# Moving weight accumulations, token sums, splits and additions in a one-core hybrid transformer layer, and tying two transposes to later product steps

## The chip, the cores and the metric

The kernel runs on one core of one Trainium2 chip. The metric is the device time of one execution in microseconds (us). The core has TensorE (PE, matrix products), VectorE (DVE), ScalarE (ACT), GpSimd (POOL) and SyncE (SP, which here only issues DMAs). PE writes into PSUM banks; everything else works in SBUF. A DMA that adds to its destination (`accum_op`) is issued by POOL, plain ones mostly by SP.

## The reference, cut to what matters

All arrays are float32; L = 1024 tokens, D = 1024, 256 context tokens, one layer.

```
h      = rms_norm(x) * (1 + sc1) + sh1          # modulated by c
r, d   = split_heads(h @ w_in)                  # 4 retention heads, 4 differential heads
y_ret  = silu(g) * (both directions of chunkwise retention, group-normed)
y_diff = subln(softmax(q1 k1) v - lam * softmax(q2 k2) v)
x      = x + g1 * (concat(y_ret, y_diff) @ w_out)
h2     = rms_norm(x) * (1 + sc2) + sh2
a, b   = split(conv3(h2 @ w_up))
x      = x + g2 * ((silu(a) * b) @ w_down)
return rms_norm(x)
```

## The kernel before, in words

**Precision.** Every large product is made from three TensorE passes (`passes`, lines 130 to 135): high by high, high by low, low by high. So each operand is split: ACT casts the high part, and DVE (or POOL) subtracts it from the raw values to give the low part. One call of `passes` is three matmuls and is called a step here; a `product` is four steps.

**Strassen forms.** The out projection (tokens times `w_out`) and the up and down projections use seven half-size products in place of eight. Their operands are sums of blocks. `A11, A12, A21, A22` are the four blocks of `w_out`; the sums of them live in DRAM: `ws_d[0] = A21 + A22`, `ws_d[1] = A11 + ws_d[0]`, `ws_d[2] = A11 + A21`, `ws_d[3] = A12 + ws_d[1]`. First SP copies one block into each (lines 808 and 810), then POOL adds the other with accumulating DMAs in two halves of 512 KB each (`weight_sum`, line 366). The sums of token blocks live in `t1_d` to `t4_d` (in the profile `sgd`), the second half of the retention rows in `yr_d` (`yrd`).

**Stages around the change.**

1. Query projection (up to about 445 us). PE makes `pl` products; beside it the generator `outputs()` runs the 16 head pairs of retention. A `Pair` loads its keys `rk` (line 257) and values `kvo` on SP, `score` makes `pc` (line 269), POOL forms `qq`, DVE `sc`, PE `po`, ACT squares, POOL takes a power (line 288), DVE normalizes (293), POOL adds and gates (295, 296), PE transposes (301), ACT copies to `yr`, and SP writes it out (309). For the second half of the tokens POOL also accumulates `yr` into `t1_d` (line 311). After some pairs `weight_sum` issues its DMAs.
2. Attention (about 445 to 650 us). 32 units (4 heads of 8 query tiles) run as a software pipeline written out by hand; in step n unit n begins its scores. Its order on PE, DVE, ACT and SP is fixed (`in_order`). POOL makes each unit's power (line 987, `pool_ins`), and issues loads and sums "after" the `pool_ins` of the unit five steps back: query and key loads for unit n + 3 (lines 1018, 1021), `joined_tokens` (an addition and one or two accumulating DMAs, lines 1130 and 1132), the copy `t2_d <- t1_d` (1150), and one slice of the out weights (`wo_gen`, line 1100). SP copies `t2_d` to `t4_d` per head at steps 14, 21 and 29 (1152).
3. Out projection (about 640 to 728 us). `out_step` makes the products; `weights` loads, casts and subtracts a block of weights (1106 and 1107), `sum_operand` does so for token sums (1336 and 1337; for `t4_d`, the last head is added up from two parts at line 1333), and `gate` multiplies a result by `g1` (1345) and adds it to `x1` (1346). Rows 0 to 3 are `rows0`, rows 4 to 7 `rows1`; `left` and `right` are column halves. `freed` is the last of the four gates of `rows0`, `left`.
4. `norm2` normalizes a finished row tile (ACT squares at 1226, DVE 115, POOL power 116, DVE scaling 1231). `turned` transposes a column of row tiles on PE (1238) into one PSUM bank, once for the first four tiles (`turned0`) and once for the last four (`turned1`); the copies out of it (1240, 1242) are split (1245 and 1246) and combined (1423, 1426) into the operands B11 to B22 and T1 to T4.
5. Up projection. The first three blocks' `chain` and `second` products stand ahead of the loop, with `turned1` beside them, one of its pieces after every few steps; then `fifth` (reads T1) and `third` (reads B22), then the `chain` products that read T2, T3, T4.

**What sets the order.** Within `in_order` sections it is the order of the program. Elsewhere a planner orders each engine's instructions when the kernel is built, from the dependencies, the order of the program and its own costs. `order_only(a, b)` tells it to put a behind b on their common engine; it makes no wait on the chip. `issue_after` does so for DMA issues. `last_turn[1, d]` is the last row tile's transpose for column d.

Of the kernel before, what the change touches and what calls it, by code (L numbers as in the profile page):

```python
# [12 lines left out]
ALU = mybir.AluOpType  # L13
# [4 lines left out]
P = 128  # L18
# [56 lines left out]
def kernel(  # L75
# [85 lines left out]
    with ExitStack() as p1:  # L161
# [89 lines left out]
        class Pair:  # L251
# [46 lines left out]
            def turn(self, behind=None):  # L298
                pt = tr_tile([P, 2, P], "pyt")
                for s in range(2):  # L300
                    ins = nc.tensor.transpose(pt[:, s, :], self.y[:, s, :], ident)
                    if behind is not None:
                        order_only(ins.ins, behind.ins)
                left = H * NT // 2 - 1 - (self.h * NT // 2 + self.g)
                yr = rt.tile([P, 2, P], F32, name="yr") if left > 1 else rt.tile([P, 2, 2, P], F32, name="yr", tag=("qq", "sc")[left])[:, 0]
                second, o = self.g // 2, self.g % 2 * 2 * P
                nc.scalar.mul(yr, pt, 1.0 if second else -1.0)
                for to in (yr_d,) if second else (t3_d, t1_d):
                    nc.sync.dma_start(out=to[:, self.h, o : o + 2 * P].rearrange("p (s l) -> p s l", s=2), in_=yr)
                if second:  # L310
                    nc.gpsimd.dma_start(out=t1_d[:, self.h, o : o + 2 * P].rearrange("p (s l) -> p s l", s=2), in_=yr, accum_op=ALU.add)

        keyed, key_copies = [], []
# [44 lines left out]
                    last[d] = dst  # L358
                yield

        w_terms = [(i, a, k) for i, a in ((0, A22), (2, A21), (1, ws_d[0]), (3, ws_d[1])) for k in (0, 2)]

        def weight_sum(after):
            if w_terms:
# [4 lines left out]
        def outputs():  # L369
            n_pairs, per_head = H * NT // 2, NT // 2  # L370
            pairs, more = {}, states((2, 3))
            for n in range(-2, n_pairs + 3):
                if n + 2 < n_pairs:
                    pairs[n + 2] = Pair(n + 2)
                if n == -2:
                    continue
                if n + 1 < n_pairs:
                    pairs[n + 1].score()
                forming = per_head <= n < 3 * per_head
                if n == per_head - 1 or forming and n % 2 == 0:  # L380
                    next(more)
                yield
                if 0 <= n < n_pairs:
                    pairs[n].output(0)
                yield
                if forming:
                    next(more)
                yield
                if n == n_pairs + 2:
                    for _ in range(4):  # L390
                        yield
                    pairs[n - 3].turn(newest[0])
                elif n >= 3:
                    pairs[n - 3].turn()
                if 0 <= n < n_pairs:
                    pairs[n].output(1)
                    pairs[n].squares()
                yield
                if 0 <= n - 1 < n_pairs:
                    pairs[n - 1].gate()  # L400
                    for _ in range({1: 2, 2: 2, 10: 1, 11: 1, 12: 1, 13: 1}.get(n, 0)):
                        weight_sum(last_y[0])
                if forming:
                    next(more)
                yield
                yield
# [684 lines left out]

    g1 = wo.tile([P, D], F32, name="g1")

    def out_weights(srcs, sl, eng=nc.sync, low=nc.vector, lag=0, after=()):
        raws = []
        srcs = [src[:, k, :] for src in srcs for k in range(4)]
        for k in range(len(srcs) + lag):
            if k < len(srcs):
                raw = wo.tile([P, 512], F32, name="woraw", bufs=5)
                wo_loads.append(eng.dma_start(out=raw, in_=srcs[k]))  # L1100
                raws.append(raw)
            yield
            if k >= lag:
                whi = wo.tile([P, 512], F32R, name="wohi", bufs=8)
                wlo = wo.tile([P, 512], F32R, name="wolo", bufs=8)
                wo_casts.append(nc.scalar.copy(whi, raws[k - lag]))
                part = low.tensor_tensor(out=wlo, in0=raws[k - lag], in1=r32(whi), op=ALU.subtract)
                for ins in after:
                    order_only(part.ins, ins.ins)
                sl.append((whi, wlo))  # L1110

# [22 lines left out]
    with ExitStack() as p2:  # L1134
        at = p2.enter_context(tc.tile_pool(name="at", bufs=2, reuse_waits="tile"))
        psa = p2.enter_context(tc.tile_pool(name="psa", bufs=1, space=PSUM, reuse_waits="tile"))

        turns = {}
        start = len(nc.cur_bb.bb.instructions)
        order = sorted(TAU.items(), key=lambda it: it[1] % 1.0)  # L1140
        for n in range(n_units + 8):
            if 2 < n < n_units:
                units[n] = Unit(n)
                vars(units[n]).update(fore[n])
            if n == 9:
                with tc.issue_after(units[n - 5].pool_ins.ins):
                    nc.gpsimd.dma_start(out=g1, in_=row_d[0].rearrange("p c -> (p c)").partition_broadcast(P))
            if n == 8:
                with tc.issue_after(units[n - 5].pool_ins.ins):
                    nc.gpsimd.dma_start(out=t2_d[:, :, :], in_=t1_d[:, :, :])  # L1150
            if n in (14, 21, 29):
                nc.sync.dma_start(out=t4_d[:, (14, 21, 29).index(n), :], in_=t2_d[:, (14, 21, 29).index(n), :])
            for half, when in ((0, (11, 18, 26, 33)), (1, (16, 24, 31))):
                if n in when:
                    with tc.issue_after(units[min(n - 5, n_units - 1)].pool_ins.ins):
                        joined_tokens(when.index(n), half)
            for op, t in order:
                u = n - int(t)
                if 0 <= u < n_units and (u > 1 or op not in EARLY) and (op, u) not in MOVED:
                    turns[op, u] = len(nc.cur_bb.bb.instructions)  # L1160
                    units[u].run(op)
                    turns[op, u] = nc.cur_bb.bb.instructions[turns[op, u]]
                for o, v in MOVED.get((op, u), ()):
                    units[v].run(o)
                if op == "f" and n >= 9 and n not in (11, 16, 18, 24, 26, 31, 33):
                    with tc.issue_after(units[min(n - 6, n_units - 1)].pool_ins.ins):
                        next(wo_gen, None)
            if n + 3 < n_units:
                after = units[n - 5].pool_ins if n >= 5 else last_va[0]
# [148 lines left out]
        for _ in g:  # L1318
            pass

    def weights(src, *after):
        sl = []
        run(out_weights((src,), sl, after=after))
        return sl

    def sum_operand(src, tt, half, turn=False, after=()):
        raw = raw0[:, 4 * half : 4 * half + 4, :]
        n = H if src is not t4_d else H - 1
        nc.sync.dma_start(out=raw[:, :n, :], in_=src[:, :n, :])
        if n < H:  # L1330
            nc.sync.dma_start(out=raw[:, 3, :], in_=t2_d[:, 3, :])
            for a in range(2):
                nc.gpsimd.tensor_tensor(out=raw[:, 3, :], in0=raw[:, 3, :], in1=r32(yT[a][1][:, D // P - 1, :]), op=ALU.add)
        sign, parts = -1.0 if turn else 1.0, []
        for k in range(H):
            cast = nc.scalar.mul(tt[0][:, k, :], raw[:, k, :], sign)
            part = nc.vector.scalar_tensor_tensor(out=tt[1][:, k, :], in0=raw[:, k, :], scalar=sign, in1=r32(tt[0][:, k, :]), op0=ALU.mult, op1=ALU.subtract)
            for ins in after:
                order_only(part.ins, ins.ins)
            parts.append(part)  # L1340
        return parts
# [37 lines left out]
    for t in range(4):  # L1379
        freed = gate(rows0[t], c1[t], left, ALU.add)  # L1380
        done(t, left)
    w4 = weights(A22, freed)
    sum_operand(t4_d, Y12, 1, after=(freed,))
    raws = [up_load(j) for j in range(NSUM)]
    halves = [(a[:, 0:4, :], a[:, 4:8, :], b[:, 0:4, :], b[:, 4:8, :]) for a, b in raws]
    for a1, a2, b1, b2 in halves:
# [12 lines left out]
    w2 = weights(A12)  # L1399
    beside(turned0(), 0.36, -3.0)  # L1400
    for t in out_step(c1, Y12, w4, False, True, True):
        gate(rows1[t], c1[t], right, ALU.subtract, nc.gpsimd)
        done(4 + t, right)
    c1 = [(psB if t < 2 else psC).tile([P, 512], F32, name=f"o3_{t}", tag="bank") for t in range(4)]
    for t in out_step(c1, Y22, w2, True, True, True):
# [62 lines left out]
    for j in range(NPRE):  # L1468
# [460 lines left out]
```

## Time and profile before

| | us |
|---|---|
| runs | 1374.64, 1375.2, 1376.37 (median 1375.2) |
| profiled execution | 1374.97 |
| its span, first to last instruction | 1373.2 |
| PE busy | 1350.2 |
| DVE busy | 1001.5 |
| ACT busy | 749.1 |
| POOL busy | 351.8 |
| mean granted TensorE clock | 0.998 of full |

In a timeline row stand the start and the length in us, the engine, the line of the kernel, the operation, what is written from what, shapes and a count; in brackets, how long the engine sat idle before it and whose end released it. Rows that merge several instructions give the time from the first start to the last end. Consecutive PE and DVE operations overlap a little, so the distance from one start to the next is shorter than an operation's length. SPq and POOLq rows are DMA issues. A row of a stretch gives for each engine its busy time and its count of instructions, then the granted clock, the mean share in which the 16 DMA engines were busy, and GB/s. A row of a wait gives the total, the number of times and the longest.

### The profile page before, as it was taken

The numbers are of one execution on the slowest core, as the hardware profiler recorded it, in microseconds if no ns is written. First come the engines' busy times: TensorE is split into PE (matmuls) and PEld (weight loads), VectorE is DVE, ScalarE is ACT, GpSimd is POOL, SyncE is SP. The second block draws the span as 40 slices with busy tenths as digits, with TensorE's granted clock in tenths as the row PEclk, the third lists the DMA queues.
The fourth block names the chain that finished last, engine by engine and source line by source line (L and its number), as shares of the span: only waits on it lengthen the run. The fifth ranks groups of instructions, "written<-read, shape, count | busy, mean of one in ns | idle before, by whom it ended". The sixth has DMA issues, their size and how long they took to land.

```text
span 1373.2 us, 19870 instructions
## 1 busy us (share of the span) xinstructions
PE 1350.2 (98%) x6978; PEld 1134.5 (83%) x6978; DVE 1001.5 (73%) x1508; ACT 749.1 (55%) x1429; POOL 351.8 (26%) x440
## 2 busy tenths in 40 slices
PE   9999999999999999999999999999999999999997
PEld 6788888888888799988877888888888888888886
DVE  4746874425775898997889986777766777798857
ACT  4643312434665789987437654455554555455543
POOL 1210005403777435543131222212222210000001
PEclk9999999999999999999999999999999999999999
DMA  9567897655877877745853898988888875963523
GB/s 362 218 252 245 288 325 232 202 171 157 212 199 189 186 168 141 145 93 154 333 165 92 200 224 218 232 223 214 208 221 215 208 193 171 375 217 110 176 92 123
DMA packets 130636, 279.71 MB, mean 204 GB/s; under 512 B 13716, under 2 KB 35220, under 8 KB 129624
## 3 DMA queue, kind: packets, MB, share of 16 engines
q1 hardware_dynamic: 100440, 212.99, 45.6%
q0 software_dynamic: 29520, 64.00, 25.4%
q10 hardware_dynamic: 576, 1.44, 0.3%
q8 instruction: 55, 0.90, 0.3%
q14 instruction: 45, 0.37, 0.1%
HBM read 212.04 MB, written 69.75 MB: 205 GB/s over the span
## 4 chain that ended last, share of the span: by engine, by line
PE 81%; DVE 7%; ACT 4%; POOL 3%; issue 3%; DMA 2%; SPq 0%; POOLq 0%; DVEq 0%; ACTq 0%
PE chain L133 6%; PE chain L134 6%; PE chain L135 6%; PE c L134 5%; PE c L133 5%; PE c L135 5%; PE pv L972 4%; PE pA L940 4%; PE pn L135 3%; PE pn L134 3%; PE pn L133 3%; PE pl L133 3%; PE pl L135 3%; PE pl L134 3%; PE third L133 3%; PE third L135 3%
## 5 line engine op out<-in xcount | busy, mean ns | idle before, releaser
L1263 POOL DMA_DIRECT2D cmb<-w_up x80 | 73.6, 1142 | 175.1 <-DMA cmb<-w_up 141.7
L133 PE MATMUL pl<-hT,whi 128*128 128x512 f32 x256 | 105.4, 412 | 0.0
L133 PE MATMUL chain<-T,whi 128*128 128x512 f32 x264 | 103.1, 391 | 0.0
L134 PE MATMUL chain<-T,whi 128*128 128x512 f32 x264 | 102.8, 389 | 0.0
L135 PE MATMUL chain<-T,wlo 128*128 128x512 f32 x264 | 102.2, 389 | 0.0
L943 DVE TENSOR_REDUCE mt<-pA 128x1 f32<-128x1280 f32 x64 | 95.2, 1488 | 7.5 <-PE pA L940 6.3
L135 PE MATMUL pl<-hT,wlo 128*128 128x512 f32 x256 | 100.1, 391 | 0.0
L134 PE MATMUL pl<-hT,whi 128*128 128x512 f32 x256 | 99.9, 390 | 0.0
L947 ACT ACTIVATE p<-pA,mt 128x1280 f32<-128x1280 f32 x64 | 85.5, 1336 | 11.2 <-DVE mt L943 9.1
L940 PE MATMUL pA<-ks,qhl 128*128 128x512 f32 (+1 forms) x384 | 89.6, 368 | 1.3 <-DMA ks<-dk 0.8
L133 PE MATMUL c<-whi,ghl 128*128 128x512 f32 x232 | 90.2, 389 | 0.0
L134 PE MATMUL c<-wlo,ghl 128*128 128x512 f32 x232 | 90.2, 389 | 0.0
L135 PE MATMUL c<-whi,ghl 128*128 128x512 f32 x232 | 90.2, 389 | 0.0
L1187 ACT CAST whi<-cmb 128x512 fp32r<-128x512 f32 x60 | 37.4, 625 | 83.0 <-PE chain L134 65.1
L940 PEld LDWEIGHTS pA<-ks,qhl 128*128 128x128 f32 x384 | 67.9, 189 | 13.7 <-DVE mt L943 1.2
L972 PE MATMUL pv<-va,aT 128*128 128x128 f32 x640 | 77.4, 276 | 1.3 <-DVE yT L1001 1.0
L972 PEld LDWEIGHTS pv<-va,aT 128*128 128x128 f32 x640 | 74.0, 192 | 3.0 <-DVE yT L1001 2.1
L1187 ACT CAST whi<-wra 128x512 fp32r<-128x512 f32 x54 | 33.0, 622 | 71.7 <-PE third L134 42.3
L134 PE MATMUL third<-yT,whi 128*128 128x512 f32 x168 | 65.4, 389 | 0.0
L133 PE MATMUL third<-yT,whi 128*128 128x512 f32 x168 | 65.4, 389 | 0.0
L135 PE MATMUL third<-yT,wlo 128*128 128x512 f32 x168 | 65.4, 389 | 0.0
L133 PE MATMUL pn<-whi,hT 128*128 128x512 f32 x160 | 64.8, 405 | 0.0
(342 smaller groups left out, 3854.6 us busy)
## 6 DMA issues: line engine op xcount, KB each, us to landing
cmb<-w_up POOLq DMA_DIRECT2D x80, 256.0 KB, 6.5
wm<-w_mod SPq DMA_DIRECT2D x32, 512.0 KB, 5.7
cmb<-w_up SPq DMA_DIRECT2D x60, 256.0 KB, 5.4
raw<-w_in SPq DMA_DIRECT2D x27, 512.0 KB, 5.4
wra<-w_up SPq DMA_DIRECT2D x23, 512.0 KB, 6.2
W<-w_down SPq DMA_DIRECT2D x44, 256.0 KB, 5.5
wrb<-w_up SPq DMA_DIRECT2D x40, 256.0 KB, 3.8
ad<-s SPq DMA_DIRECT2D x20, 512.0 KB, 5.8
```

The source lines that it names most:

```text
L133: mm(ps, lh, rh, start=first, stop=False, skip_group_check=more)
L134: mm(ps, lh, rl, start=False, stop=False, skip_group_check=more)
L135: return mm(ps, ll, rh, start=False, stop=last, skip_group_check=more)
L940: mm(self.pa[m][:, c0:c1], self.q[:, m, i, qs], self.k[:, m, c0:c1], start=(i == 0), stop=(i == 1))
L943: nc.vector.tensor_reduce(out=self.mt[:, m : m + 1], in_=self.pa[m][:, :LK], axis=AX.X, op=ALU.min)
L947: nc.scalar.activation(self.p[m], self.pa[m][:, :LK], AF.Exp, scale=-1.0, bias=self.mt[:, m : m + 1], accum_out=self.s[:, m : m + 1])
L972: mm(self.pv, self.aT[:, c, :], self.v[:, c, :], start=(c == 0), stop=(c == NKT - 1))
L1187: cast = nc.scalar.copy(hi, src)
L1263: nc.gpsimd.dma_start(out=o, in_=src, accum_op=ALU.add)
```

## The change

- The four accumulations `ws_d[1] += ws_d[0]` and `ws_d[3] += ws_d[1]` are issued no longer after pairs 9 to 12 but in steps 15, 17, 21 and 28 of attention.
- The last head's two accumulations of `yr` into `t1_d` are left out; step 6 of attention does both at once, from `yr_d`, in DRAM. The copy `t2_d <- t1_d` goes from step 8 to 9, the first join from 11 to 12; a weight slice is taken at 11 and not at 12.
- For the fourth block of out weights (`w4`) and for `t4_d`, the first two of four subtractions need not follow `freed`.
- Six additions go from POOL to DVE: two in `sum_operand`, four in the gates of `rows1`, `right`.
- The transposes `last_turn[1, 0]` and `last_turn[1, 4]` were put behind the third and fourth step of block 0's `second`; they are put behind the second and third step of block 1's `chain`.

```diff
-                if second:
+                if second and self.h < H - 1:
                     nc.gpsimd.dma_start(out=t1_d[...], in_=yr, accum_op=ALU.add)
...
-        w_terms = [(i, a, k) for i, a in ((0, A22), (2, A21), (1, ws_d[0]), (3, ws_d[1])) for k in (0, 2)]
+        w_terms = [(i, a, k) for i, a in ((0, A22), (2, A21)) for k in (0, 2)]
...
-                    for _ in range({1: 2, 2: 2, 10: 1, 11: 1, 12: 1, 13: 1}.get(n, 0)):
+                    for _ in range({1: 2, 2: 2}.get(n, 0)):
...
-    def out_weights(srcs, sl, eng=nc.sync, low=nc.vector, lag=0, after=()):
+    def out_weights(srcs, sl, eng=nc.sync, low=nc.vector, lag=0, after=(), free=0):
...
-                for ins in after:
+                for ins in after if k - lag >= free else ():
                     order_only(part.ins, ins.ins)
...
-            if n == 8:
+            if n in (6, 9, 15, 17, 21, 28):
                 with tc.issue_after(units[n - 5].pool_ins.ins):
-                    nc.gpsimd.dma_start(out=t2_d[:, :, :], in_=t1_d[:, :, :])
+                    if n == 6:
+                        nc.gpsimd.dma_start(out=t1_d[:, H - 1, :], in_=yr_d[:, H - 1, :], accum_op=ALU.add)
+                    elif n == 9:
+                        nc.gpsimd.dma_start(out=t2_d[:, :, :], in_=t1_d[:, :, :])
+                    else:
+                        i, j, k = {15: (1, 0, 0), 17: (1, 0, 2), 21: (3, 1, 0), 28: (3, 1, 2)}[n]
+                        nc.gpsimd.dma_start(out=ws_d[i][:, k : k + 2, :], in_=ws_d[j][:, k : k + 2, :], accum_op=ALU.add)
...
-            for half, when in ((0, (11, 18, 26, 33)), (1, (16, 24, 31))):
+            for half, when in ((0, (12, 18, 26, 33)), (1, (16, 24, 31))):
...
-                if op == "f" and n >= 9 and n not in (11, 16, 18, 24, 26, 31, 33):
+                if op == "f" and n >= 9 and n not in (12, 16, 18, 24, 26, 31, 33):
...
-    def sum_operand(src, tt, half, turn=False, after=()):
+    def sum_operand(src, tt, half, turn=False, after=(), free=0):
...
-                nc.gpsimd.tensor_tensor(out=raw[:, 3, :], in0=raw[:, 3, :], in1=..., op=ALU.add)
+                nc.vector.tensor_tensor(out=raw[:, 3, :], in0=raw[:, 3, :], in1=..., op=ALU.add)
...
-            for ins in after:
+            for ins in after if k >= free else ():
                 order_only(part.ins, ins.ins)
...
-    w4 = weights(A22, freed)
-    sum_operand(t4_d, Y12, 1, after=(freed,))
+    w4 = weights(A22, freed, free=2)
+    sum_operand(t4_d, Y12, 1, after=(freed,), free=2)
...
-        gate(rows1[t], c1[t], right, ALU.subtract, nc.gpsimd)
+        gate(rows1[t], c1[t], right, ALU.subtract)
...
-        if j == 0:
-            order_only(last_turn[1, 0].ins, steps[-2].ins)
-            order_only(last_turn[1, 4].ins, steps[-1].ins)
+        if j == 1:
+            order_only(last_turn[1, 0].ins, steps[-7].ins)
+            order_only(last_turn[1, 4].ins, steps[-6].ins)
```

More of the change, by code (lines that the diff above doesn't have):

```diff
@@ L1319, in run, with weights @@
             pass
-    def weights(src, *after):
+    def weights(src, *after, free=0):
         sl = []
-        run(out_weights((src,), sl, after=after))
+        run(out_weights((src,), sl, after=after, free=free))
         return sl
-    def sum_operand(src, tt, half, turn=False, after=()):
+    def sum_operand(src, tt, half, turn=False, after=(), free=0):
         raw = raw0[:, 4 * half : 4 * half + 4, :]
@@ L1332, in sum_operand @@
             for a in range(2):
-                nc.gpsimd.tensor_tensor(out=raw[:, 3, :], in0=raw[:, 3, :], in1=r32(yT[a][1][:, D // P - 1, :]), op=ALU.add)
+                nc.vector.tensor_tensor(out=raw[:, 3, :], in0=raw[:, 3, :], in1=r32(yT[a][1][:, D // P - 1, :]), op=ALU.add)
         sign, parts = -1.0 if turn else 1.0, []
```

## The prediction

> **What bounds the kernel now.** I read the page's first parts, then TensorE's waits over the whole span, then the timelines of each engine around each wait, then rows by stage.
>
> ```profile
> span 1373.2 us, 19870 instructions
> ...
> PE 1350.2 (98%) x6978; PEld 1134.5 (83%) x6978; DVE 1001.5 (73%) x1508; ACT 749.1 (55%) x1429; POOL 351.8 (26%) x440
> ```
>
> TensorE (PE) is busy in 1350.2 of 1373.2 us: 23.0 us idle is all that a reordering can win.
>
> ```profile
> PE pt L1238 <- DVE x L1231: 4.1, 4, 1.7
> PE pc L269 <- DMA rk<-rk: 1.8, 1, 1.8
> PE pt L960 <- DVE xa L462: 1.1, 1, 1.1
> PE pA L940 <- DMA ks<-dk: 0.8, 1, 0.8
> PE pt L1238 <- DVE sm L115: 0.8, 1, 0.8
> ```
>
> The columns are the total, the count and the longest wait in us. Of these rows the change can reach the first (4.1), the second (1.8), the fourth (0.8) and the fifth (0.8): 7.5 us together. The third belongs to the hand-over to attention, whose chain of DVE operations is not edited.
>
> The profiled execution took 1374.97 us, 1.77 over its span; the median of the runs is 1375.2, so the sum below stands 0.2 under the median. What a measurement of this kernel can tell from no change is about 0.2%, 2.75 us: 1372.4 to 1378.0.
>
> **Weight accumulations out of the query projection.** Four POOL DMAs (`wsd<-wsd`, 512 KB each, read, added and written back) leave the stage in which the head pairs run.
>
> ```profile
> 400.00:410.00 10.00, 8.02 (x50) 6.51 (x49) 5.38 (x14) 4.12 (x14) 7.21 (x9) 1.00 1.01 242
> 398.89 0.86 POOL L366 DMA_DIRECT2D wsd<-wsd  x1
> 399.49 1.32 POOL L288 TENSOR_TENSOR ss<-ss,mhalf 128x4 f32<-128x4 f32 x1
> 402.94 0.73 POOL L296 TENSOR_TENSOR y<-y,kvo 128x256 f32<-128x256 f32 x1
> 403.61 0.88 POOL L366 DMA_DIRECT2D wsd<-wsd  x1
> 404.11 0.43 SPq L257 DMA_DIRECT2D rk<-rk  x1
> 408.44 0.68 PE L269 MATMUL pc<-xa,rk 128*128 128x128 f32 x4 [1.80 <-DMA rk<-rk]
> DMA to landing us min/median/max: 2.0/3.8/8.7
> ```
>
> The first row is a stretch of 10 us: DMA share 1.01, PE busy 8.02. PE waits 1.80 us at 408.44 for the keys `rk`, issued by SP at 404.11. That issue stands on SP behind a load whose buffer is released by the POOL multiply at 402.94; that multiply stands behind DVE and POOL work delayed by the accumulation at 398.89. The next POOL instruction starts 0.60 after it, at 399.49, so I move the `rk` issue 0.6 us earlier. The keys took at most 408.44 - 404.11 = 4.3 us to land, with two accumulations in flight beside the rope table, `kvo` and `yr`; the quickest of the sixteen `rk` loads took 2.0. To cost nothing it must land by 406.64, which is 3.1 us after the earlier issue. The median, 3.8, leaves 0.7 of wait; the minimum leaves none. Bounds: gain 1.1 to 1.8, and, if the rope table alone fills the queues, 0.6. I take 1.5, between median and minimum, because the median itself was taken beside full queues.
>
> By the Trainium skill ("DMA: Bandwidth & Descriptors", section "Anatomy of one DMA — SWDGE (gpsimd) path") a transfer issued by POOL takes about 2.0 us plus its bytes over 436 GB/s; used as an estimate for this 128 KB load that is 2.3 us, no wait would be left, and the sum would be 0.3 lower. The measured 4.3 us shows what the fit leaves out, the transfers beside it.
>
> The other two accumulations (409.94 and 417.70 on POOL) end no PE wait: nothing.
>
> **Last head's token sum.** Two POOL accumulations go; one DRAM-to-DRAM accumulation at step 6 of attention replaces them.
>
> ```profile
> 435.21 0.95 POOL L311 DMA_DIRECT2D sgd<-yr  x1
> 437.23 0.88 POOL L311 DMA_DIRECT2D sgd<-yr  x1 [0.44 <-DMA yrd<-yr]
> 440.04 1.38 POOL L1021 DMA_DIRECT2D ks<-dk  x2
> 449.16 1.40 PE L940 MATMUL pA<-ks,qhl 128*128 128x512 f32 x6 [0.83 <-DMA ks<-dk]
> ```
>
> They stand in front of the first attention loads. Without them the `ks` pair at 440.04 is issued 1.6 us earlier (0.60 of POOL for each, as above, and the 0.44 that the second waited), and the queues hold 256 KB of read-modify-write less. PE's wait of 0.83 at 449.16 is smaller than that: it goes. Lower bound 0, if the other loads of the same queue fill the place; I take 0.8, as the issue gain is twice the wait. Late next is the third row of the waits, DVE `xa` (1.1): it follows from these scores through DVE, so it moves with them and I count neither gain nor loss.
>
> **What enters attention.** Five accumulations at steps 6, 15, 17, 21, 28, the copy `t2<-t1` one step later, the first join and one weight slice swapped between 11 and 12.
>
> ```profile
> 563.01 0.56 POOL L987 TENSOR_TENSOR ssa<-ssa,mhalf 128x1 f32<-128x1 f32 x1 [4.42 <-DVE ssa L986]
> 568.77 0.57 POOL L987 TENSOR_TENSOR ssa<-ssa,mhalf 128x1 f32<-128x1 f32 x1 [3.83 <-DVE ssa L986]
> qhl<-dq POOLq DMA_DIRECT2D x14, 512.0 KB, 6.5
> wsd<-wsd POOLq DMA_DIRECT2D x4, 512.0 KB, 8.4
> L1100 SPq DMA_DIRECT2D woraw<-wsd x12: 319/320/669, 635.1 to 672.3; - x12
> DMA to landing us min/median/max: 3.3/7.4/10.7
> ```
>
> One unit is 568.77 - 563.01 = 5.76 us. POOL waits 3.83 us for DVE before the second of these rows, and step 21's accumulation is issued just behind the first: one issue (0.86 to 0.90 above) fits. Late on POOL would be the `pow`, then the norm on ACT; with 3.8 us of cover it costs 0, and 0.9 each if the cover were gone (4.5 for five). The join at 12 adds nothing new, and SP's copy of `t4` at step 14 waits for it with nothing needed behind. A query load lands in 6.5 us and is issued three units, 17.3 us, ahead: 10.8 us of slack against 8.4 for an accumulation in front of it. Each new accumulation waits on POOL for what it reads: step 6 for writes that ended before attention, the copy at 9 for step 6 (17.3 us, against 8.4), steps 21 and 28 for those at 15 and 17; none holds the queue. Step 28 falls six units after the second row, near 603, and lands by 614 (10.7 at most, the landing line of these sums); SP's loads of them begin at 635.1. Taken: 0, bounds 0 and +4.5.
>
> **Splits of the fourth out weights and tokens (`free=2`).** Two `wolo` and two `yT` subtractions need no longer follow the last gate `freed`.
>
> ```profile
> 684.12 0.60 ACT L1106 CAST wohi<-woraw 128x512 fp32r<-128x512 f32 x1
> 687.21 1.37 DVE L1345 TENSOR_TENSOR gated<-o,g 128x512 f32<-128x512 f32 x2 [3.04 <-PE o L135]
> 692.10 2.49 DVE L1107 TENSOR_TENSOR wolo<-woraw,wohi 128x512 fp32r<-128x512 f32 x4
> 694.51 2.49 DVE L1337 SCALAR_TENSOR_TENSOR yT<-raw,yT 128x512 fp32r<-128x512 f32 x4
> 710.67 0.33 PE L1238 MATMUL pt<-ident,x 128*128 128x128 f32 x1 [1.66 <-DVE x L1231]
> ```
>
> DVE idles 3.04 us up to 687.21, and its backlog from 692.10 to 696.92 is eight operations at 0.60 (2.41 for four). The casts they need exist by 684.7 (the row on ACT is the second `wohi`). Four move into the hole: the gates of the next step start 2.4 us earlier. At the end of that chain PE waits 0.21 and 1.66 us for the normalized rows, 1.87 in all. Bounds: 0 (the planner leaves them behind) to 1.87; I take 1.8, because 2.4 covers it. Late next would be PE's own order: nothing.
>
> **POOL adds to DVE.** Two adds for the last head's sum, four gate adds.
>
> ```profile
> 677.62 2.99 POOL L1333 TENSOR_TENSOR raw<-raw,yT 128x512 f32<-128x512 f32 x2 [27.97 <-DMA raw<-sgd]
> 711.70 4.09 POOL L1346 TENSOR_TENSOR x<-x,gated 128x512 f32<-128x512 f32 x3
> 679.40 1.77 DVE L1107 TENSOR_TENSOR wolo<-woraw,wohi 128x512 fp32r<-128x512 f32 x1
> 713.34 0.69 DVE L1345 TENSOR_TENSOR gated<-o,g 128x512 f32<-128x512 f32 x1 [1.13 <-POOL x L1346]
> L1246 DVE TENSOR_TENSOR yT<-raw,yT 128x512 fp32r<-128x512 f32 x3 | 4.8, 1638 | 0.1
> ```
>
> On DVE each costs 0.60: 1.2 and 2.4 us. But while POOL's adds run, DVE's own two-input operations stretch: the three `L1246` took 1638 ns on average, where an operation of this size takes 0.68 (2.49 us for the four at 692.10, started 0.60 apart), 2.9 us lost; the `wolo` at 679.40 took 1.77. And DVE waited 1.13 for POOL at 713.34. So the gate adds give 2.4 - 2.9 - 1.1 = -1.6 us, and the two others 1.2 - 1.1 (1.77 - 0.68) = about 0. These two have further cover in the hole, which holds 3.04 + 1.1 against 2.4 + 1.2. If the stretching has another cause, DVE pays 3.6 us instead.
>
> **Second half's rows and the tied transposes.**
>
> ```profile
> 730.93 0.33 PE L1238 MATMUL pt<-ident,x 128*128 128x128 f32 x1 [0.83 <-DVE sm L115]
> 732.71 0.33 PE L1238 MATMUL pt<-ident,x 128*128 128x128 f32 x1 [1.45 <-DVE x L1231]
> 737.64 0.33 PE L1238 MATMUL pt<-ident,x 128*128 128x128 f32 x1 [0.79 <-DVE x L1231]
> 738.00:764.00 26.00, 26.00 (x128) 21.35 (x127) 25.69 (x43) 21.48 (x37) 6.21 (x7) 1.00 0.59 127
> ```
>
> DVE reaches the norms of rows 4 to 7 by 2.4 (moved) + 1.6 = 4.0 us sooner, of which 1.87 is used up by PE coming sooner: 2.1 net. The first two waits, 0.83 + 1.45 = 2.28, shrink to 0.2 at best. The third, 0.79, stands before the last row's transpose, which now comes two steps of a product later (6 matmuls at 26.00/128 = 0.20, 1.2 us): gone. That is at best 2.9. DVE in this stretch also waits for ACT squares and POOL powers, which don't shrink; I take 2.0. Bounds: 0.8 (the tie alone) to 3.1.
>
> What the tie puts off is the chain from this transpose to T1 to T4: in the last row DVE is busy in 25.69 of 26 us, no room to catch up, while PE arrives up to 2.9 us earlier and the chain only about 1.7 (2.9 less 1.2). The product with the last T1 slice can be put behind others, but the order is fixed at build: I take back 0.6, bounds 0 and 1.2.
>
> **Sum.** 1374.97 - 1.5 - 0.8 - 0 - 1.8 - 0 - 2.0 + 0.6 = 1369.5 us, 0.4% under the median. With every reachable wait gone: 1374.97 - 7.5 = 1367.5.
>
> **Rivals.**
>
> *The row stages net nothing.* The planner orders DVE anew; if the freed splits stay behind the gates or the stretching returns in another pair, only the two DMA waits go: 1374.97 - 2.3 = 1372.7, within the 0.2%. For: DVE's 25.69 of 26 us. Against: the 3.04 us hole.
>
> *Slower: DVE's full stretch starts late.* Place: the chain behind the last row's transposes. If the six adds cost their 3.6 us with nothing returned, and the tie holds the chain by another 1.8 (three steps, 9 matmuls at 0.20), PE waits 5.4 us more in the T products, where every microsecond is passed on. Less 2.3: 1374.97 + 3.1 = 1378.1. It decides when the chain starts more than 2.3 us later, counted from attention's end, than now. Against: the lost 2.9 us on the very rows that ran beside POOL.
>
> *Attention pays.* The accumulations take the queues from a query load. With two in front, 6.5 + 2 x 8.4 - 17.3 = 6.0 us of PE wait, which takes the gain back: 1375.5. Decides when a load lands over 17.3 us after its issue. Against: they are spaced two units or more apart.
>
> The Trainium skill (same page, section "Issuing engines are not separate DMA queues") says that transfers of all issuing engines interleave on the same 16 DMA engines; by it the moved bytes cost the same wherever they run. The DMA share of 1.01 beside a PE wait agrees; no row here shows a PE wait for a load within attention.
>
> *The DMA waits stay* (the rope table fills the queues): the row stages alone, 1374.97 - 3.2 = 1371.8, still faster.
>
> **How the numbers follow.** Likeliest 0.54, with its own range 1367.5 to 1371.8; DMA waits stay 0.12; row stages nothing 0.17; attention pays 0.06; slower 0.11. Faster: 0.54 + 0.12 and a little of the third, 0.68. Same: the rest of the third and attention, 0.21. Slower 0.11. The range leaves out the slow case (0.11) above and under a tenth below: 1367.0 to 1376.0.
>
> **What would show it.** Right: no `pc<-rk` wait near 408 and no `pA<-ks` wait near 449; the DVE idle before the gates at 687 filled with `wolo` and `yT`; `L1246` near 684 ns throughout; the transposes' waits below 1 us in all; POOL still waiting for DVE before every `pow`. Wrong: a new PE wait at the `fifth` or `third` products for DVE's T rows, a PE wait for `qhl` or `ks` in attention, or gates of the last rows later on DVE than now.

## The result and the profile after

The changed kernel takes 1366.3 us (median of six runs, 1365.3 to 1367.5) against 1375.05 for the kernel before beside it (1373.7 to 1376.7). The ratio is 0.9935, interval 0.9922 to 0.9948: 8.8 us less, where 5.5 were forecast. It is outside the forecast range by 0.7 us, on the fast side.

Its profiled execution took 1365.33, with this span and these busy times (page, first part):

```profile
span 1363.5 us, 19850 instructions
...
PE 1348.6 (99%) x6978; PEld 1134.9 (83%) x6978; DVE 998.3 (73%) x1514; ACT 749.6 (55%) x1429; POOL 341.7 (25%) x433
```

PE has the same 6978 matmuls, and 14.9 us of idle time in place of 23.0. Of TensorE's waits (total, count, longest) these stand where the quoted five stood, with two others that matter below:

```profile
PE pt L960 <- DVE xa L462: 0.7, 1, 0.7
PE pv L972 <- DVE yT L1001: 0.5, 2, 0.2
PE pt L1244 <- DVE x L1237: 0.4, 1, 0.4
PE chain L135 <- DVE wlo L1197: 0.2, 1, 0.2
```

`rk`, `ks` and `sm` are gone, 4.1 us for `x` became 0.4. The two stretches of the DMA waits (PE's busy time is the first number behind the length, the DMA share the last but one):

```profile
400.00:410.00 10.00, 10.00 (x68) 8.96 (x67) 6.43 (x14) 5.27 (x18) 7.21 (x7) 1.00 0.58 193
440.00:450.00 10.00, 10.00 (x48) 8.33 (x48) 5.73 (x6) 4.54 (x7) 4.11 (x4) 1.00 0.90 237
```

PE is busy throughout; at 400 the DMA share fell from 1.01 to 0.58. At 440 the kernel before had:

```profile
440.00:450.00 10.00, 9.17 (x42) 7.33 (x41) 3.08 (x4) 3.28 (x6) 4.91 (x7) 1.00 1.17 281
```

On DVE the hole in front of the gates, 3.04 us before, is filled with two `wolo`, two `yT` and the two adds (L1339) that came from POOL; 0.88 us of idle time is left:

```profile
677.13 0.69 DVE L1107 TENSOR_TENSOR wolo<-woraw,wohi 128x512 fp32r<-128x512 f32 x1
677.73 0.69 DVE L1339 TENSOR_TENSOR raw<-raw,yT 128x512 f32<-128x512 f32 x1
678.34 0.69 DVE L1343 SCALAR_TENSOR_TENSOR yT<-raw,yT 128x512 fp32r<-128x512 f32 x1
...
681.70 1.37 DVE L1351 TENSOR_TENSOR gated<-o,g 128x512 f32<-128x512 f32 x2 [0.88 <-PE o L135]
```

Where the time went is seen from the starts of the same instruction in both traces. The stages end at: the score product `pc` near 401 and the last one near 414; the first and the last transposed attention output (`pty`); the first `chain` product of up; the first `fifth`; the last `chain` product that reads a T slice; the end. Four executions of the kernel before (its own profile and runs e13 to e15 below) and two of the changed kernel (its own and e16), in us:

| stage | before | after | middle values differ by | forecast |
|---|---|---|---|---|
| start to 401 | 401.1, 400.3, 400.3, 401.6 | 400.3, 400.5 | -0.3 | 0 |
| last two pairs' scores | 13.6, 18.6, 13.4, 12.8 | 11.1, 11.1 | -2.4 | -1.5 |
| hand-over to attention | 60.7, 59.6, 61.6, 61.6 | 59.6, 59.6 | -1.6 | -0.8 |
| attention | 174.9, 174.9, 174.9, 174.9 | 174.3, 174.2 | -0.6 | 0 |
| out projection | 77.4, 76.4, 76.2, 76.4 | 74.6, 75.0 | -1.6 | -1.8 |
| rows 4 to 7 | 23.9, 24.4, 24.4, 23.8 | 20.9, 21.0 | -3.1 | -2.0 |
| T products | 403.7, 403.8, 403.8, 403.7 | 404.4, 404.4 | +0.7 | +0.6 |
| rest | 217.9, 218.0, 217.9, 217.9 | 218.2, 218.2 | +0.4 | 0 |

Before rounding the differences add up to 8.6 us. Within one kernel attention, the T products and the rest repeat to 0.2 us, so that even small differences count there. In the kernel before, the two stages with waits for DMAs spread by 5.8 and 2.1 us, the start and the out projection by 1.3, rows 4 to 7 by 0.6. The hand-over alone overlaps with that of the changed kernel; together with the scores in front of it, it does not (74.3, 78.1, 75.0 and 74.5 against 70.7 twice).

### The profile page after: what moved, and what is told of

Same layout as the page of the kernel before. It is cut to its first block, busy times and chain, and to the rows that moved or that the text cites. A ratio compares the mean times of both kernels' runs of the same rounds, so it can differ in the third digit from the quotient of the medians.

```text
span 1363.5 us, 19850 instructions
## 1 busy us (share of the span) xinstructions
PE 1348.6 (99%) x6978; PEld 1134.9 (83%) x6978; DVE 998.3 (73%) x1514; ACT 749.6 (55%) x1429; POOL 341.7 (25%) x433
## 4 chain that ended last, share of the span: by engine, by line
PE 87%; DVE 5%; ACT 3%; issue 2%; DMA 1%; POOL 1%; POOLq 0%; DVEq 0%; ACTq 0%
PE chain L135 6%; PE chain L133 6%; PE chain L134 6%; PE c L134 5%; PE c L133 5%; PE c L135 5%; PE pv L972 4%; PE pl L133 4%; PE pl L135 4%; PE pl L134 4%; PE pA L940 4%; PE pn L135 3%; PE pn L134 3%; PE pn L133 3%; PE third L134 3%; PE third L133 3%
```

## The experiments

**DMA edits alone, row edits alone.** The first kernel keeps rows, adds, splits and ties as before, the second the DMAs.

```diff
 e1:  -    w4 = weights(A22, freed, free=2)        # and the adds and the tie back
      +    w4 = weights(A22, freed)
 e2:  -        w_terms = [(i, a, k) for i, a in ((0, A22), (2, A21)) for k in (0, 2)]
      +        w_terms = [... ((0, A22), (2, A21), (1, ws_d[0]), (3, ws_d[1])) ...]
```

> The kernel before with the edits of the DMAs alone: weight accumulations and last head's token sum in attention, the copy at step 9, the join at 12; the splits, the additions and the two tied transposes as before. Theory (the parts add up, and a TensorE wait costs its recorded idle time plus some 0.2 us of restart): the waits for rk (1.80), S (0.18), ks (0.83) and parts of two later ones (0.4 and 0.5) go, 3.7 us of idle and about 0.6 of restarts, 4.0 to 4.5 us under the kernel before, near 1370.8; the transposes' waits of the row stages (4.9 us in all) stay as they were. Rival (only the recorded idle is lost, and keys and first scores alone gain): 2.6 us, near 1372.4. Rival (the row stages' gain hangs on the DMAs too): 6 us or more, and the transposes' waits shrink.

> The kernel before with the edits of the row stages alone: the two freed splits of weights and tokens, six additions on VectorE, the two transposes behind later steps; all DMAs as before. Theory (the parts add up): the waits before the transposes, 4.9 us of idle before, fall to about 0.4, with some 0.2 us of restart for each of five waits: 4.5 to 5.3 us under the kernel before, near 1370.2; the waits for rk (1.8) and ks (0.8) stay. Rival (recorded idle alone): 4.5. Rival (these edits gain only once the weights come earlier): under 3 us.

Measured: 1368.7 us, ratio 0.9962 (0.9950 to 0.9975), and 1370.3, 0.9972 (0.9962 to 0.9982): 5.2 and 3.8 us less, 9.0 together. Both halves gain, and nearly add up; e1 gave more than the 4.0 to 4.5 expected, e2 less than its 4.5 to 5.3. By stages e1 has the scores at 11.1, the hand-over at 59.6 and attention at 174.2, as in the changed kernel, and the rows at 23.8, as before; e2 the reverse (out projection 74.7, rows 20.9, T products 404.4), but its scores took 15.9. That is this wait in its list of waits, and the stretches behind it:

```profile
PE pc L269 <- DMA rk<-rk: 2.5, 1, 2.5
```

```profile
408.00:410.00 2.00, 1.28 (x6) 1.14 (x7) 1.97 (x3) 0.00 (x0) 1.92 (x3) 0.83 1.07 221
410.00:412.00 2.00, 2.00 (x11) 1.90 (x9) 1.31 (x2) 1.76 (x8) 1.70 (x2) 0.50 1.06 304
412.00:414.00 2.00, 2.00 (x10) 1.64 (x10) 1.01 (x3) 0.67 (x3) 1.03 (x1) 0.82 0.96 158
```

The number after POOL's is the granted clock: 2 x (0.17 + 0.50 + 0.18) = 1.7 us lost behind 2.50 us of idle time.

**The tie, undone and alone.**

```diff
 e3:  -        if j == 1:                          # in the changed kernel
 e3:  -            order_only(last_turn[1, 0].ins, steps[-7].ins)
 e3:  +        if j == 0:
 e3:  +            order_only(last_turn[1, 0].ins, steps[-2].ins)
 e12: the same lines the other way round, in the kernel before
```

> The changed kernel with the two transposes tied as before (third and fourth step of block 0's second product). Theory (the tie removes only the wait for the last row tile): the 0.79 us wait comes back, with its restart 0.8 to 1.1 us over the changed kernel, near 1367.3; the waits for the fifth to seventh row tile stay gone. Rival (the tie carries most of the second half's gain of 2.8 us): 2 us or more over it, near 1368.5. Rival (the rows are now early enough without it): no difference.

> The kernel before with only the tie of the last row's transposes changed. Theory (what the tie gains in the row stage is given back behind the T rows): the wait of 0.79 us near 737 goes, the stage up to the first product with T1 is 0.8 to 1.0 us shorter, the stretch from there to the last product with a T slice 0.7 us longer; no change in time, ratio 0.999 to 1.001. Rival (the tie's gain stays, as the prediction's lower bound of 0.8 had it): 0.8 us faster, and the stretch behind the first T1 product is not longer.

Measured: 1365.8, ratio 0.9939 (0.9927 to 0.9952), the changed kernel's time; and 1375.8, ratio 1.0009 (1.0000 to 1.0018). Neither shows a gain from the tie. Rows 4 to 7 take 21.8 without it against 21.0, the T products 403.6 against 404.4; all eight kernels here with the new tie have 404.4 or 404.5, all others 403.6 to 403.8. In e12 rows 4 to 7 took 24.6 and not the 0.8 to 1.0 less that was expected: the wait of 0.79 us near 737 is gone, but the granted clock was 0.83 from 730 to 740, where the first profile of the kernel before had 1.00; without the tie that wait is gone too where the clock fell there (e13, e14). Most of the price in the T products is paid at one place, where the first product with T meets its split weights:

```profile
752.64 0.39 PE L134 MATMUL chain<-T,whi 128*128 128x512 f32 x1
753.20 0.50 PE L135 MATMUL chain<-T,wlo 128*128 128x512 f32 x1 [0.17 <-DVE wlo L1197]
753.54 0.39 PE L133 MATMUL chain<-T,whi 128*128 128x512 f32 x1
```

Matmuls start 0.23 us apart; here one starts 0.56 after the one in front, and the next 0.34 after it: 0.44 us lost of the 0.7, of which the waits view shows 0.17.

**The six adds back on POOL.**

```diff
-        nc.vector.tensor_tensor(out=raw[:, 3, :], ...)
-        gate(rows1[t], c1[t], right, ALU.subtract)
+        nc.gpsimd.tensor_tensor(out=raw[:, 3, :], ...)
+        gate(rows1[t], c1[t], right, ALU.subtract, nc.gpsimd)
```

> The changed kernel with the six additions on GpSimd again; TensorE's order is the same instruction for instruction. Theory (GpSimd's additions stretch VectorE's two-input operations beside them, so moving them is free on VectorE): the row splits beside them take over 1200 ns in the mean instead of 684, 2 to 3 us are lost on VectorE, and the waits before the transposes come back by 1 to 2.5 us: 1367.3 to 1369. Rival (the splits moved into the hole are enough by themselves): within 0.5 us of the changed kernel, with the stretched operations in the trace all the same.

Measured: 1367.4, ratio 0.9952 (0.9938 to 0.9966), 1.1 us over the changed kernel by the medians, with intervals that overlap; rows 4 to 7 took 22.3 against 21.0, 1.3 us. The splits of one shape (min, median, max in ns) show the stretching, in the changed kernel and in this one:

```profile
L1252 DVE TENSOR_TENSOR yT<-raw,yT x12: 679/684/692, 706.2 to 743.3; 128x512 fp32r<-128x512 f32 x12
```

```profile
L1252 DVE TENSOR_TENSOR yT<-raw,yT x12: 677/682/1827, 706.1 to 744.4; 128x512 fp32r<-128x512 f32 x12
```

The median is the same; the two that ran beside POOL's adds took up to 1827 ns.

**All splits behind the last gate.**

```diff
-    w4 = weights(A22, freed, free=2)
-    sum_operand(t4_d, Y12, 1, after=(freed,), free=2)
+    w4 = weights(A22, freed)
+    sum_operand(t4_d, Y12, 1, after=(freed,))
```

> The changed kernel, but all eight splits of the fourth out weights and tokens follow the last gate again. Theory (the freed splits carry the out projection's gain of 2.9 us): TensorE waits again 1.5 to 2.1 us for the normalized rows near 705 to 715, the out projection is 2 to 2.8 us longer than in the changed kernel, the time 1.5 to 2.8 us over it, ratio to before 0.9945 to 0.9955. Rival (the two adds moved to DVE and the earlier start carry it, the freed splits nothing): within 0.5 us of the changed kernel, ratio 0.993 to 0.994.

Measured: 1367.6, ratio 0.9951 (0.9937 to 0.9964). That is 1.3 us over the changed kernel by the medians, with intervals that overlap. The stage tells more: the out projection took 76.7, as before (76.2 to 77.4), against 74.6 and 75.0; PE waits again:

```profile
PE pt L1244 <- DVE x L1237: 1.7, 1, 1.7
```

The freed splits carry the gain of this stage; the two moved adds alone give none.

**Weight accumulations alone, token sum alone.**

```diff
 e5:  only the w_terms and step 15, 17, 21, 28 lines of the change
 e10: only the `self.h < H - 1` line, step 6, and the copy and join one step later
```

> The kernel before with only the four weight accumulations moved from the head pairs into attention; last head's token sum, splits, adds and transposes as before. Theory (the two DMA waits stand in for each other, since the ks loads are not released by TensorE's progress alone): the wait for rk near 408 goes, which brings attention 2.0 to 2.5 us nearer, but the wait for ks near 449 grows from 0.83 to 1.5 to 3; the kernel is 0.3 to 1.5 us faster than before, ratio 0.999 to 0.9998. Rival (independent terms, as the prediction summed them): rk goes, ks stays 0.8, 2.0 to 2.5 us faster, ratio 0.9982 to 0.9985.

> The kernel before with only the last head's token sum moved into attention (with the copy and the first join one step later); the weight accumulations stay in the head pairs. Theory (the two waits stand in for each other): the wait for rk stays 1.8 to 2.5, the wait for ks goes and the wait for xa is 0.7 instead of 1.1; 1.0 to 2.0 us faster than before, and with weights alone and token sum alone together less than the 5.6 of both DMA edits. Rival (the ks loads are held by the weight accumulations' bytes, not by the token sum): ks stays 0.8, no change in time.

Measured: 1371.1, ratio 0.9976 (0.9967 to 0.9985), 3.3 us less; and 1372.1, 0.9986 (0.9977 to 0.9995), 1.9 less. Together 5.2, what both give in e1 (each is known to about 1.2 us). So the theory that the two waits stand in for each other fell: with the weights moved, the wait for `ks` stayed 0.7 us, and with the token sum moved, the wait for `rk` stayed (0.9) and that for `ks` went. In the profiled execution of e5 the clock fell once more, behind 1.4 us of idle time for `xa`:

```profile
458.00:460.00 2.00, 0.60 (x6) 0.36 (x4) 2.00 (x3) 0.79 (x2) 1.56 (x3) 1.00 0.94 266
460.00:462.00 2.00, 1.53 (x7) 1.07 (x7) 2.00 (x3) 1.57 (x5) 0.00 (x0) 0.93 0.69 233
462.00:464.00 2.00, 2.00 (x12) 1.78 (x10) 2.00 (x2) 1.15 (x3) 1.27 (x1) 0.50 0.04 8
464.00:466.00 2.00, 2.00 (x14) 2.00 (x14) 1.32 (x4) 2.00 (x4) 0.00 (x0) 0.72 0.49 194
```

**The accumulations in place with an eighth of their bytes.** The other seven eighths of these sums are left out.

```diff
-  added = nc.gpsimd.dma_start(out=ws_d[i][:, k : k + 2, :], in_=a[:, k : k + 2, :], accum_op=ALU.add)
+  n = 512 if i in (0, 2) else 64
+  added = nc.gpsimd.dma_start(out=ws_d[i][:, k : k + 2, :n], in_=a[:, k : k + 2, :n], accum_op=ALU.add)
```

> The kernel before with the four weight accumulations of the head pairs in their place and number, but with 64 of 512 columns each, 64 KB instead of 512 KB; that part of the weight sums is left out. In the trace of the kernel before, the keys that TensorE waits for at 408.44 were issued at 399.86, 0.97 us behind the accumulation at 398.89, and took 8.4 us to land; with the accumulations elsewhere the same load takes 3.9 to 4.1. Theory (the bytes of the accumulation hold the load up): the load lands in 3.7 to 4.7 us, the wait for rk goes, the stage is 2.0 to 2.5 us shorter up to the last pair; the wait for ks near 449 grows, and the kernel is 0.3 to 3 us faster. Rival (the prediction's: POOL's issue of 0.6 us stands in front and delays the load's issue): the issue has not moved, the load takes over 7 us and TensorE waits 1.2 to 1.8 us as before, no change in time.

Measured: 1376.4, ratio 1.0007 (0.9998 to 1.0016). The load of the keys issued near 399 took, from issue to landing, before, after, and in this kernel:

```profile
DMA to landing us min/median/max: 8.4/8.4/8.4
```

```profile
DMA to landing us min/median/max: 3.9/3.9/3.9
```

```profile
DMA to landing us min/median/max: 4.6/4.6/4.6
```

The bytes hold the load up, and the wait for `rk` was gone. But no time came with it: PE then waited 1.1 us for `yr` on ACT and 0.9 for `qq` on POOL, where an accumulation's issue took 1.20 us:

```profile
404.12 1.20 POOL L367 DMA_DIRECT2D wsd<-wsd  x1
404.93 1.72 POOL L266 TENSOR_TENSOR qq<-st,qd 128x512 f32<-128x512 f32 x1
```

This suggests that the place on POOL costs too, and that only the move takes both away. It is not shown: part of it may belong to the small rows of this kernel's accumulations, whose issue took 1.20 us where the same one took 0.88 before.

**The keys later on purpose.** In the changed kernel, small loads on the key tile in front of the last pair's key load, which must wait for them: one (e7), one that waits for POOL's roots (e8), three in a row (e11).

```diff
+                if n == H * NT // 2 - 1:
+                    for _ in range(3):
+                        nc.sync.dma_start(out=self.k[0:1, 0, 0:4], in_=gn[0:1, 0, 0:4])
                 nc.sync.dma_start(out=self.k, in_=rk_d[self.h][...])
```

> The changed kernel with a 16-byte load into the last pair's key tile in front of its key load on the same tile, so that the key load can only start when it has landed, about 2 us later. A wait of 1 to 2 us for rk is put back into TensorE's stretch near 405, with everything else in its place. Theory (a wait costs its recorded idle plus 0.2 to 0.3 us, because the modelled end of the matmul in front of it lies 0.16 us behind the place where the next could have started, and the first matmuls behind it start further apart): from the first score product of the pair in front to the first matmul of attention the stretch grows by the recorded idle plus 0.2 to 0.3. Rival (recorded idle is the whole price): it grows by the recorded idle within 0.1. Time 1.2 to 2.3 us over the changed kernel.

> The changed kernel, the small load now reading the roots that POOL makes near 404.2, so that the key load starts about 4 us later than in the changed kernel and TensorE waits 2.7 to 3.7 us for it. Theory (an idle time of 2.5 us or more is followed by a stretch at a lower granted clock, as in the kernel that kept the DMAs in place, where 2.50 us were followed by matmuls at twice the pitch for 3 us; 1.80 us before were not): the granted clock falls to about 0.5 for some 3 us behind the wait, and the stretch grows by the idle plus 1.7 to 2.1 us, the time by 4.5 to 6 over the changed kernel. Rival (that drop was an accident of one execution): the clock stays at 1.00 and the stretch grows by the idle plus 0.3, the time by 3 to 4.

> The changed kernel with three small loads in a row on the key tile in front of the last pair's key load; the key load starts near 409.5 and TensorE, which needs it at 411.0, waits 1 to 2 us. Theory (a wait costs its recorded idle plus 0.2 to 0.3): without a fall of the granted clock, the stretch from the score product near 405 to attention's first matmul grows from 37.1 us by the idle plus 0.2 to 0.3, and the time is 1.2 to 2.3 us over the changed kernel; with a fall of the clock (it fell after 1.40 us of idle in one kernel and did not after 1.80 in another) by 1.7 to 2.1 more. Rival (recorded idle is the whole price): it grows by the idle within 0.1.

Measured: 1366.0 (ratio 0.9940, 0.9927 to 0.9954), 1371.1 (0.9978, 0.9969 to 0.9987), 1369.9 (0.9966, 0.9953 to 0.9978). The expectations of e7 and e8 put the need for these keys near 405; it is at 411, so e7 made no wait and tells nothing but that 2 us of slack are there. In e8 the roots that the small load read were those begun at 411.13, not the ones near 404, and the key load was issued at 413.90, 11.5 us later than in the changed kernel and not 4; that its wait lies within the 2.7 to 3.7 us expected was luck. In e11 the key load was issued at 410.54 and not near 409.5, and the wait is longer than the 1 to 2 us expected. The two waits, e11 and e8:

```profile
413.84 0.68 PE L272 MATMUL pc<-xa,rk 128*128 128x128 f32 x4 [2.38 <-DMA rk<-rk]
```

```profile
416.12 1.04 PE L273 MATMUL pc<-xa,rk 128*128 128x128 f32 x4 [3.15 <-DMA rk<-rk]
```

From the score product near 405 to attention's first matmul the changed kernel takes 37.1 us (442.33 - 405.20), e11 41.3 (446.67 - 405.39), e8 42.0 (447.81 - 405.77). That is 4.2 and 4.9 more, for 2.38 and 3.15 of idle time. In e11 the granted clock was, per stretch:

```profile
414.00:415.00 1.00, 1.00 (x9) 1.00 (x9) 0.44 (x1) 0.58 (x3) 1.00 (x2) 0.85 0.06 16
415.00:418.00 3.00, 3.00 (x11) 2.52 (x11) 2.38 (x3) 0.00 (x0) 3.00 (x3) 0.50 0.39 44
418.00:419.00 1.00, 1.00 (x9) 0.89 (x8) 0.72 (x2) 0.35 (x1) 0.25 (x1) 0.95 0.00 0
```

(1 - 0.85) + 3 x (1 - 0.50) + (1 - 0.95) = 1.7 us of lost clock, and 2.38 + 1.7 = 4.1. In e8 it was 0.57 from 416 to 420, again 1.7 us, and 3.15 + 1.7 = 4.9. So a wait's price is its idle time and the clock lost behind it; of the 0.2 to 0.3 us that I expected besides, at most 0.1 is left at this size. At 753, where the wait was short, they did show (0.44 for 0.17).

**Both kernels once more.**

> The kernel before, unchanged, for the spread of its stages between executions (first of three). Theory (the prediction's terms were read from one execution, whose waits vary by about 1 us from the next one, and the granted clock falls in some executions): over the three, the wait for rk lies between 0.9 and 2.5 us, the stretch from the last T-free score product near 401 to attention's first turned output between 73.5 and 75.5, the out projection between 76.0 and 77.5, the second half's rows at 23.8, or 24.4 to 24.7 where the clock falls near 735. Rival (the stages repeat within 0.2 us and the terms were wrong in kind): 74.4, 77.5 and 23.8 each time.

> The kernel before, unchanged, second of three; expectation as for the first.

> The kernel before, unchanged, third of three; expectation as for the first.

> The changed kernel, unchanged, once more. Theory (with the waits gone nothing is left to vary): 70.7, 74.6 to 75.4 and 20.8 to 21.0 us for the same three stretches, no fall of the clock before the last 20 us, the waits as in its first profile. Rival: a wait for rk or ks comes back in some executions, and one of the stretches is 1 us or more longer.

Measured: the stage table above. The key load took 11.3, 8.2 and 7.6 us in the three executions of the kernel before (8.4 in its first profile), and 4.1 in the changed one (3.9). In e13 PE waited 4.62 us for them (the profile names ACT's cast, but the keys landed at 399.01 + 11.3 = 410.3):

```profile
410.43 1.20 PE L269 MATMUL pc<-xa,rk 128*128 128x128 f32 x4 [4.62 <-ACT xhl L448]
```

The clock fell in these stretches (the number after POOL's):

```profile
400.00:410.00 10.00, 5.61 (x35) 4.34 (x33) 5.91 (x14) 3.60 (x11) 7.24 (x9) 0.90 1.02 242
410.00:420.00 10.00, 9.57 (x50) 8.69 (x51) 3.90 (x7) 5.02 (x20) 5.74 (x7) 0.76 0.75 180
730.00:740.00 10.00, 7.75 (x30) 5.88 (x29) 8.07 (x18) 5.68 (x11) 2.05 (x3) 0.83 0.26 93
```

In e14 it fell near 735 alone, in e15 and in the changed kernel nowhere ahead of the last 20 us. The theory held, but for e13, where 2.5 us of wait were the most that it allowed. The changed kernel repeats to 0.4 us in each stage.

## Why the prediction was right, and where it was wrong

The direction was right and the size too small: the stages gave 8.6 us where the sum had 5.5, and the time fell under the range. Of the 3.1 us between them rows 4 to 7 bring 1.1, the scores 0.9, the hand-over 0.8 and attention 0.6; the other stages take 0.3 back. The lower end of the range lay just under a ceiling that was none. The steps that failed follow by name.

**Right.** The direction, and four of the five named signs: no wait for `rk` near 408 nor for `ks` near 449, the hole before 687 filled, the splits at 684 ns throughout, one transposing wait of 0.37 us (under 1 us in all). The fifth, POOL waiting for DVE before every `pow`, held for 29 of 32. No PE wait for a load came within attention. The freed splits were put at 1.8 us and gave 1.6 (e6 takes 1.9 back). The T chain was put at +0.6 and took +0.7. The two-input stretching on DVE is caused by POOL's adds, as e4 shows.

**Wrong: the step "Weight accumulations out of the query projection".** It put PE's wait at 408.44 down to the keys "issued by SP at 404.11" and took 4.3 us for their way. The keys of that pair are loaded two pairs ahead: they were issued at 399.86, and SP's queue shows it, with the rope table in front:

```profile
399.38 0.39 SPq L236 DMA_DIRECT2D rtab<-rope  x1
399.86 0.43 SPq L257 DMA_DIRECT2D rk<-rk  x1
```

That load stood 0.97 us behind the accumulation at 398.89 and took 8.4 us, up to 408.3. The one at 404.11 took 8.5 us and landed near 412.6, behind the product that was to wait for it. In the changed kernel it is issued as early against PE's work (0.92 us ahead of the score product at 399.96; before 0.95 ahead of 400.81) and takes 3.9. So the 0.6 us of POOL's issue, on which the sum stood, had no part in it; the gain is 4.5 us of transfer time, all of the wait goes, and the stage gives 2.4 us, not 1.5. The median and the minimum of the sixteen loads, between which the value was chosen, were the wrong rows: the load beside the accumulation had its own.

**Mis-sized: "Last head's token sum" and what follows it.** 0.8 became 1.6, by the middle of a stage that spreads by 2.1. The wait for `xa`, which the prediction counted as neither gain nor loss, went from 1.1 to 0.7 us, and the hand-over of the kernel before took 61.6 in two of three later executions, 0.9 more than in the one that the sum used. With the token sum alone (e10) the stage took 60.4, 0.7 under the middle value before; the rest came only with the weight accumulations moved too.

**Mis-sized: "Second half's rows and the tied transposes".** 2.0 became 3.1, the upper bound as it stood (2.9 against the execution that the sum used; in two others the stage took 24.4, with the clock down). The prediction held back 0.9 for ACT squares and POOL powers "which don't shrink"; of PE's waits behind them 0.4 us is left. By the experiments the adds are worth 1.3 there (e4; put at about 0, with their gain in the rows' term) and the tie 0.8 (e3), which the T chain takes back. The tie's +0.6 there was counted, so the sum was right on it; that the tie as a whole nets about zero was not said.

**Missed: "What enters attention", costed at 0 with a bound of +4.5.** Attention became 0.6 us shorter, in every kernel with the weight accumulations moved (174.1 to 174.6) and in none without (174.8 or 174.9). PE's wait for `yT` fell from 1.0 to 0.5; how the accumulations lead to that was not found. The rest of the kernel grew by 0.4, also unexplained.

**Missed: the ceiling.** "With every reachable wait gone: 1367.5" was no bound. It took off four rows of waits of one execution and had no term for the clock. In e13 the same kernel waited 4.6 us for the same keys and lost 10 x 0.10 + 10 x 0.24 = 3.4 us of clock around that wait; in e13 and e14 the clock fell near 735 as well. A change that takes a varying wait away gains its mean with what follows it. And attention became shorter, which no row of that sum held.

## What to carry to other kernels

Pair a wait with its load by the buffer's depth, not by the nearest issue in front: with two buffers the tile waited for was asked for two turns ago. Look then at what was issued just before that load on any queue; here a 512 KB accumulation doubled its way. And take a second execution before a sum of waits is called a ceiling: here attention and the T products repeated to 0.2 us, while the two stages that waited for DMAs spread by 5.8 and 2.1.

## What the runs showed of the hardware

- The granted clock fell to 0.50, and not by the length of PE's idle time alone. It fell with waits of 2.38 (e11), 2.50 (e2), 3.15 (e8) and 4.62 us (e13), after 1.40 and 0.47 us (e5, at 460), and after 0.8 and 1.45 us near 735 in e9, e10, e12, e13 and e14. It did not after 1.80 us (before, at 408), nor after the same 0.8 and 1.45 us in the first profile of the kernel before, in e1, e5 and e15. A fall cost 1.7 us in e2, e8 and e11, which is 3.4 us at half clock, and twice that in e13. Near 735 rows 4 to 7 took only 0.6 us more, 24.4 against 23.8, as the next wait, 0.79 us, was gone then. The Trainium skill ("TensorE: Matmul & The Clock Gate", section "What's actually happening") has a free-running activity window, which fits a fall that depends on where the idle time lies; it names one idle window of about 3.4 us as the condition, and here 1.4 us, with a shorter wait close behind, were enough.
- A 128 KB load issued just behind a 512 KB accumulation took 7.5 to 11.3 us in seven executions, against 3.7 to 4.5 in nine without it, with the rope table in flight in both; with 64 KB in the accumulation it took 4.6. The estimate of 2.3 us quoted in the prediction from the Trainium skill ("DMA: Bandwidth & Descriptors", section "Anatomy of one DMA — SWDGE (gpsimd) path") was short of all of them.
